# Splitting the short TensorE products of an attention block into three parts

## The chip, the cores and the metric

The kernel runs on one core of one Trainium2 chip. The metric is the device time of one execution in microseconds (us). Three runs of the kernel before gave 789.17, 789.42 and 789.59 us, median 789.42.

## The reference

One layer of a transformer trunk over 512 positions of width 2048: a normalisation, windowed attention with 32 query heads and 4 key/value heads, a gated output projection, a gated embedding, and a last normalisation. All of it is computed in single precision; the kernel writes each factor as a high and a low half and adds three products for one.

```
hn = rmsnorm(x, norm_g[i])
q, k, v, gate = split(hn @ w_in)
scores = einsum('bnqhgd,bnjhd->bnhgqj', q, kb) * HEAD_DIM ** -0.5 + bias
scores = where(mask, scores, min)
m = maximum(scores.max(-1), sink)
e = exp(scores - m)
probs = e / (e.sum(-1) + exp(sink - m))
out = einsum('bnhgqj,bnjhd->bnqhgd', probs, vb)
x = x + (out * silu(gate)) @ w_out
...
g = sigmoid(rmsnorm(x, ple_norm[i]) @ ple_gate[i])
x = x + (p[i] @ ple_proj[i]) * g
return rmsnorm(x, final_g)
```

## The kernel before

The program has four stretches. The first makes the keys, the values and the first two query tiles. The second, which the change is in, makes the other 14 query tiles and all 16 gate tiles by the generator `projections` and runs attention beside them. The third is the output projection, the fourth the gate of the embedding and the last normalisation.

A tile of the second stretch is made in 16 steps of the contraction. One step, advanced by `ksteps(1)`, is a call of `mm3`: three products whose moving side is 128x512 (lines 124, 125 and 126: high by high, low by high, high by low). These are called the long products here. Eight steps use one weight tile `wraw` of 128x1024, which ScalarE casts to its high half `whi` (`W.high`, line 107) and VectorE turns into its low half `wlo` (`W.low`, line 113). A cast is made when `splits(2)` finds fewer than two tiles ready past the one in use; it reads `at`, the number of steps issued so far.

Attention is cut into 64 blocks (4 key/value heads, 16 blocks of 32 positions each). The loop `for i in range(blocks + 3)` is a software pipeline written by hand. In turn `i` TensorE runs:

- `turn(i - 2)`, line 483: two transposes of the probabilities of block i-2 into the bank `pt`, 128x128 each;
- `weigh(i - 3)`, lines 527 and 529: the probabilities of block i-3 by the values, two products of 128x256 into the bank `o`, and a third (`own` by `DV`) for blocks whose window is cut within a tile, 48 of the 64;
- `scores(i)`, line 405: two products of queries by keys into the bank `s`, 128x288 in most blocks;
- then `todo` steps of the projections, 6 in the first 20 turns and 7 afterwards.

The first three are called the short products. Around them, in the same turn: `biased(i)` (VectorE, lines 443 to 456) adds the bias to the scores and takes the row maximum `sm`; `exps(i)` and, one turn later, `shares(i)` (ScalarE, lines 465 and 475) make the probabilities, with `inverse(i)` (VectorE, line 469) between; `high(i - 2)` (ScalarE, line 488) and `low(i - 2)` (VectorE, line 496) split the transposed probabilities into `r`; GpSimd cuts `own` out of `r` (line 507); `cross` and `merge` (lines 542 and 551) put the result away; `place(i)` (GpSimd, lines 416 to 425) clears the tile `t`. When a tile of the projections ends, its result is taken out by `evac_q` (line 277) or `evac_gate` (lines 574 and 575), issued by `ksteps` right after the last step. The scores' bank `s` exists once, the banks of `pt`, `o` and the projections twice.

TensorE and SyncE follow the order of the code throughout, and the other engines do so in this stretch: each engine's queue holds its instructions in the order in which the loop issues them. SyncE's queue carries the weight loads (line 101) and copies of weights within HBM (line 677), GpSimd's the additions onto those copies (line 679).

Of the kernel before, what the change touches and what calls it, by code (L numbers as in the profile page):

```python
# [55 lines left out]
def trunk_kernel(ctx: ExitStack, tc: tile.TileContext, a: dict):  # L56
# [26 lines left out]
    def bank(name, tag):  # L83
        return others.get(tag, psum).tile([P, 512], F32, tag=tag, name=name)
# [4 lines left out]
    class Weights:  # L89
# [13 lines left out]
        def high(self):  # L103
            i = len(self.made)
            self.load(min(i + 3, len(self.srcs)))
            hi, lo = (wpool.tile([P, WE], F32R, tag=f"w{v}", name=f"w{v}{i}") for v in ("hi", "lo"))
            nc.scalar.copy(hi, self.raw[i])  # L107
            self.made.append(tuple(t.rearrange("p (k c) -> p k c", k=8) for t in (hi, lo)))
            self.open.append((lo, self.raw[i], hi))
# [268 lines left out]
    def load_bias(kv):  # L378
        biases[kv] = apool.tile([P, P + HB], F32, tag="bias", name=f"bias{kv}", bufs=2)
        src = bass.AP(  # L380
            tensor=tdram.tensor, offset=tdram.offset + GROUP * kv * TOEP + HB, ap=[[TOEP, GROUP], [1, QB], [1, P + HB]]
        )
        nc.sync.dma_start(biases[kv], src)

    def where(i):

        kv, j = divmod(i, STEPS)
        g, half = divmod(j, 2)
        return kv, j, g, 2 * half

    def scores(i):

        kv, j, g, s = where(i)
        if j == 8 and kv + 1 < KVH:
            load_bias(kv + 1)
        key = K[kv]
        q = Q[i // 4]
        s_ps = SP[i] = spsum.tile([P, 2, S], F32, tag="w", name=f"s{i}")  # L400
        n = (HB, P)[g] if g < 2 else P + QB
        for u in range(2):
            st = q[:, (2 * i + u) % (P // QB)].rearrange("p h q -> p (h q)")
            first = 0 if g < 2 else (g - 2) * HB + (s + u) * QB
            nc.tensor.matmul(s_ps[:, u, : 2 * n], st, key[:, :, first : first + n], start=True, stop=True)  # L405

    SP = {}

    def place(i):

        kv, j, g, s = where(i)
        odd = g % 2
        n = (HB, P)[g] if g < 2 else P + QB
        t = T[i] = apool.tile([P, 2, 4 + P + HB], F32, tag="t", name=f"t{i}", bufs=4)
        sink = 193 if odd else 0
        nc.gpsimd.tensor_copy(t[:, :, sink], sinkb[:, kv : kv + 1].to_broadcast([P, 2]))
        if g == 0:
            nc.gpsimd.memset(t[:, :, 65:129], MASKED)
        elif g >= 2:
            fold = HB if odd or s else 2 * QB  # L420
            if s:
                nc.gpsimd.memset(t[:, :, 1 : 1 + (s + 1) * QB], MASKED)
            else:
                nc.gpsimd.memset(t[:, 1, 1 : 1 + QB], MASKED)
            nc.gpsimd.memset(t[:, :, 1 + s * QB + n : 1 + P + fold], MASKED)

    def views(i):

        t, odd = T[i], where(i)[2] % 2
        return (t[:, :, 65:194], t[:, :, 65:193]) if odd else (t[:, :, 0:129], t[:, :, 1:129])  # L430

    def biased(i):

        kv, j, g, s = where(i)
        odd = g % 2
        n = (HB, P)[g] if g < 2 else P + QB
        t, s_ps, bias = T[i], SP.pop(i), biases[kv][:, ::-1]
        seen, pr = views(i)
        if g < 2:
            out = pr[:, :, :n]  # L440
            for u in range(2):
                at = (2 - g) * HB - (s + u) * QB
                nc.vector.tensor_add(out[:, u], s_ps[:, u, :n], bias[:, at : at + n])
            nc.vector.tensor_add(out, s_ps[:, :, n : 2 * n], out)
        else:
            fold = HB if odd or s else 2 * QB
            w = t.shape[-1]
            at = 1 + s * QB
            out = t[:, 0, at : at + n]
            out = bass.AP(tensor=out.tensor, offset=out.offset, ap=[out.ap[0], [w + QB, 2], [1, n]])  # L450
            nc.vector.tensor_add(out, s_ps[:, :, :n], bias[:, :n].unsqueeze(1).to_broadcast([P, 2, n]))
            nc.vector.tensor_add(out, s_ps[:, :, n : 2 * n], out)
            ends = t[:, :, 1 : 1 + fold], t[:, :, 129 : 129 + fold]
            nc.vector.tensor_max(ends[odd], ends[0], ends[1])
        sm = SM[i] = apool.tile([P, 8], F32, tag="sm", name=f"sm{i}", bufs=4)
        nc.vector.tensor_reduce(sm[:, 0:2], seen, axis=AX.X, op=ALU.max, negate=True)  # L456
# [14 lines left out]
    def shares(i):  # L471

        pr, sm = views(i)[1], SM.pop(i)
        for u in range(2):
            nc.scalar.mul(pr[:, u], pr[:, u], sm[:, 4 + u : 5 + u])

    def turn(i):

        pr = views(i)[1]
        T.pop(i)  # L480
        pt = PT[i] = bank(f"pt{i}", "t")[:, :256]
        for u in range(2):
            nc.tensor.transpose(pt[:, u * P : (u + 1) * P], pr[:, u, :], ident)  # L483

    def high(i):

# [27 lines left out]
    def weigh(i):  # L514

        kv, j, g, s = where(i)
        n, b = divmod(g, 2)
        r, own = PT.pop(i)
        if j == 0:
            U[kv] = apool.tile([P, 4, S], F32, tag="u", name=f"u{kv}", bufs=2)  # L520
        if j % 2 == 0:
            O[kv] = bank(f"o{i}", "o").rearrange("p (g u e q) -> p g u e q", u=4, e=2, q=QB)
        ops = O[kv]
        out = ops[:, s : s + 2].rearrange("p g u e q -> p (g u e q)")
        first = V[0 if n == 0 else n - 1 + b][:, kv]
        for low in range(2):
            nc.tensor.matmul(out, first, r[:, low], start=low == 0, stop=own is None and low == 1)  # L527
        if own is not None:
            nc.tensor.matmul(
                out, DV[:, n - 1, b, kv * 2 * HD : (kv + 1) * 2 * HD], own, start=False, stop=True  # L530
            )

    sides = [(slice(0, 64), slice(64, 128)), (slice(64, 128), slice(0, 64))]
    TMP = {}

    def cross(i):

        kv, j, g, s = where(i)
        if s:
            tmp = TMP[i] = apool.tile([P, 4, 4, QB], F32, tag="tmp", name=f"tmp{i}", bufs=1)  # L540
            for e, (o, x) in enumerate(sides):
                nc.scalar.copy(tmp[o], O[kv][x, :, :, e, :])
# [426 lines left out]
    blocks = KVH * STEPS  # L969
    at = 0  # L970

    def ksteps(n):
        nonlocal at
        for _ in range(n):
            while len(W.made) <= min(at // 8, len(W.srcs) - 1):
                W.split()
            at += 1
            next(proj)

    def splits(ahead):  # L980
        return len(W.made) <= min(at // 8 + ahead, len(W.srcs) - 1)
# [13 lines left out]
    left = KC * len(kinds) - at  # L995

    def both(f, *v):
        fill.append((partial_of(f, *v, False), partial_of(f, *v, True)))

    for i in range(blocks + 3):  # L1000

        if i % 4 in (0, 1) and 4 <= i + 4 - i % 4 < blocks:
            both(make_q, i // 4 + 1, i % 4)
            fill.insert(0, fill.pop())
        if i in (5, 20, 36):
            both(make_key, 1 + i // 16)
        if len(due) > sum(d is gate_value for _, d in fill):
            fill.append((None, gate_value))
        now = fill[:2]
        del fill[:2]  # L1010
        while W.open:
            W.low()
        if 2 <= i < blocks + 2:
            turn(i - 2)
        if 3 <= i:
            weigh(i - 3)
        if i < blocks:
            scores(i)
            place(i)
        if 2 <= i < blocks + 2:  # L1020
            high(i - 2)
        if 3 <= i:
            cross(i - 3)
        if 1 <= i < blocks + 1:
            shares(i - 1)
        for act, dve in now:
            if act:
                act()
        if i < blocks:
            biased(i)  # L1030
        if 2 <= i < blocks + 2:
            low(i - 2)
        if 3 <= i:
            merge(i - 3)
        for act, dve in now:
            dve()
        if i < blocks:
            exps(i)
            first_chores(i)
        if splits(2):  # L1040
            W.high()
        if i < blocks:
            inverse(i)
        todo = left // (blocks + 2 - i) if i < blocks + 2 else 0
        left -= todo
        ksteps(todo)
        if i < blocks:
            for n in range(i * SUM_REST // blocks, (i + 1) * SUM_REST // blocks):
                sum_weights(SUM_START + n)
# [202 lines left out]
    for at, step in enumerate(OUT):  # L1252
# [12 lines left out]
        else:  # L1265
            p, jj, m = step
# [145 lines left out]
    for at, step in enumerate(PLE, len(OUT)):  # L1412
# [15 lines left out]
        else:  # L1428
            p, jj, m = step
# [120 lines left out]
    n = done[3]  # L1550
# [87 lines left out]
```

## Time and profile before

| | us |
|---|---|
| median of three runs | 789.42 |
| the profiled execution | 789.93 |
| its span, first to last instruction | 788.2 |
| TensorE busy | 777.6 |
| first pair of transposes of the loop to the last | 105.8 to 445.6 |

A busy share of TensorE near 100% does not by itself say that it runs at its best pace: products overlap, and a product of 128x512 is shown as 0.39 us long while the next one starts 0.23 us after it. The distance between starts is what a product costs, so the views used below are lists of instructions in order of time. There the first column is the start, the second the length, and `x2` joins two equal instructions that follow each other.

### The profile page before, as it was taken

The page shows a single profiled execution, that of the slowest core. Times are in us where ns is not written, and L with a number is a line of the kernel's source. Part 1 is how long each engine was busy: PE and PEld are TensorE (multiplying, and loading weights), DVE is VectorE, ACT ScalarE, POOL GpSimd, SP SyncE. Part 2 cuts the span into 40 slices and gives each one's busy share as a digit, 9 for nine tenths or more (in the row PEclk, how much of TensorE's full clock was granted, in tenths as well). Part 3 has the DMA queues.
Part 4 walks back from the last instruction along what each step waited for, and adds up shares of the span by engine and source line. Part 5 has one row for each costly group of instructions (what it writes and reads, how often), then busy time and mean ns, then how long its engine had stood idle before and what let it go on. Part 6 is the DMA issues. An engine that isn't in the chain of part 4 may idle for free.

```text
span 788.2 us, 11280 instructions
## 1 busy us (share of the span) xinstructions
PE 777.6 (99%) x3724; PEld 648.9 (82%) x3724; DVE 619.5 (79%) x1051; ACT 507.9 (64%) x1027; POOL 185.3 (24%) x394
## 2 busy tenths in 40 slices
PE   9999999999999999999999999999999999999995
PEld 8888888888888888888888888888888888878785
DVE  4436478887877788687887798999798988989685
ACT  5723377666666666565766656767788867867465
POOL 0201514554344414443143300100000122101000
PEclk9999999999999999999999999999999999999998
DMA  8799999999999999989997597998797999967833
GB/s 335 280 202 281 301 273 327 288 298 267 312 293 261 282 281 273 270 210 278 268 241 198 146 368 262 271 378 261 238 314 215 357 244 253 259 212 217 262 109 121
DMA packets 50634, 206.99 MB, mean 263 GB/s; under 512 B 7264, under 2 KB 8416, under 8 KB 44208
## 3 DMA queue, kind: packets, MB, share of 16 engines
q1 hardware_dynamic: 40240, 156.15, 56.3%
q0 software_dynamic: 9904, 49.61, 33.1%
q8 instruction: 29, 0.48, 0.2%
q10 hardware_dynamic: 432, 0.52, 0.2%
q14 instruction: 29, 0.24, 0.1%
HBM read 199.38 MB, written 78.69 MB: 353 GB/s over the span
## 4 chain that ended last, share of the span: by engine, by line
PE 90%; DMA 3%; DVE 3%; issue 2%; ACT 1%; ACTq 0%; DVEq 0%
PE gps L124 7%; PE gps L125 7%; PE gps L126 7%; PE qps L124 7%; PE qps L125 7%; PE qps L126 7%; PE o L126 5%; PE o L124 5%; PE o L125 5%; PE g L125 3%; PE g L126 3%; PE g L124 3%; PE s L405 2%; PE o L527 2%; PE vps L246 2%; PE pt L483 2%
## 5 line engine op out<-in xcount | busy, mean ns | idle before, releaser
L507 POOL TENSOR_SCALAR_AFFINE_SELECT own<-r 64x256 fp32r<-64x256 f32 x96 | 62.2, 648 | 163.2 <-DVE r L496 81.6
L124 PE MATMUL gps<-xh,whi 128*128 128x512 f32 x256 | 100.4, 392 | 0.0
L125 PE MATMUL gps<-xl,whi 128*128 128x512 f32 x256 | 100.0, 391 | 0.0
L126 PE MATMUL gps<-xh,wlo 128*128 128x512 f32 x256 | 99.8, 390 | 0.0
L113 DVE TENSOR_TENSOR wlo<-wraw,whi 128x1024 fp32r<-128x1024 f32 x60 | 73.8, 1231 | 26.1 <-ACT whi L107 24.7
L124 PE MATMUL qps<-xh,whi 128*128 128x512 f32 x224 | 87.5, 391 | 0.0
L125 PE MATMUL qps<-xl,whi 128*128 128x512 f32 x224 | 87.5, 390 | 0.0
L126 PE MATMUL qps<-xh,wlo 128*128 128x512 f32 x224 | 87.3, 390 | 0.0
L465 ACT ACTIVATE t<-t,sm 128x129 f32<-128x129 f32 x128 | 50.7, 397 | 50.7 <-DVE sm L456 47.5
L107 ACT CAST whi<-wraw 128x1024 fp32r<-128x1024 f32 x60 | 62.3, 1038 | 16.5 <-DMA wraw<-in_w_q 12.9
L715 DVE TENSOR_TENSOR blo<-braw,bhi 128x1024 fp32r<-128x1024 f32 x43 | 52.5, 1224 | 17.4 <-ACT bhi L714 17.4
L714 ACT CAST bhi<-braw 128x1024 fp32r<-128x1024 f32 x43 | 45.0, 1048 | 30.6 <-PE g L126 9.0
L715 DVE TENSOR_TENSOR blo<-ring,bhi 128x1024 fp32r<-128x1024 f32 x48 | 58.2, 1220 | 4.3 <-ACT bhi L714 3.8
L714 ACT CAST bhi<-ring 128x1024 fp32r<-128x1024 f32 x48 | 50.2, 1049 | 17.1 <-PE o L126 13.3
L125 PE MATMUL g<-blo,fhg 128*128 128x512 f32 x148 | 58.1, 392 | 0.5 <-DVE blo L715 0.5
L124 PE MATMUL g<-bhi,fhg 128*128 128x512 f32 x148 | 58.0, 392 | 0.0
L126 PE MATMUL g<-bhi,flg 128*128 128x512 f32 x148 | 57.6, 390 | 0.0
L488 ACT CAST r<-pt 128x256 fp32r<-128x256 f32 x64 | 23.8, 372 | 51.6 <-PE pt L483 51.3
L126 PEld LDWEIGHTS gps<-xh,wlo 128*128 128x128 f32 x256 | 48.1, 188 | 10.5
L124 PEld LDWEIGHTS gps<-xh,whi 128*128 128x128 f32 x256 | 48.1, 188 | 9.1
L125 PEld LDWEIGHTS gps<-xl,whi 128*128 128x128 f32 x256 | 48.1, 188 | 8.7
L126 PEld LDWEIGHTS qps<-xh,wlo 128*128 128x128 f32 x224 | 42.1, 188 | 9.0
(298 smaller groups left out, 2033.4 us busy)
## 6 DMA issues: line engine op xcount, KB each, us to landing
w_out<-in_w_out POOLq DMA_DIRECT2D x32, 512.0 KB, 9.2
wraw<-in_w_gate_in SPq DMA_DIRECT2D x32, 512.0 KB, 7.1
ring<-w_out SPq DMA_DIRECT2D x32, 512.0 KB, 5.3
wraw<-in_w_q SPq DMA_DIRECT2D x28, 512.0 KB, 8.9
braw<-in_ple_gate SPq DMA_DIRECT2D x22, 512.0 KB, 5.3
ring<-in_w_out SPq DMA_DIRECT2D x18, 512.0 KB, 5.5
ple_gate<-in_ple_gate SPq DMA_DIRECT2D x16, 512.0 KB, 9.5
ple_gate<-in_ple_gate POOLq DMA_DIRECT2D x16, 512.0 KB, 8.1
```

The lines of the kernel that those rows point to most:

```text
L107: nc.scalar.copy(hi, self.raw[i])
L113: nc.vector.tensor_sub(lo, raw, hi.bitcast(F32))
L124: nc.tensor.matmul(ps, sh, mh, start=first, stop=False, skip_group_check=more)
L125: nc.tensor.matmul(ps, sh, ml, start=False, stop=False, skip_group_check=more)
L126: nc.tensor.matmul(ps, sl, mh, start=False, stop=last, skip_group_check=more)
L246: nc.tensor.matmul(v_ps[t], h[:, c], both[:, :, 256:512], start=f, stop=e, skip_group_check=True)
L405: nc.tensor.matmul(s_ps[:, u, : 2 * n], st, key[:, :, first : first + n], start=True, stop=True)
L465: nc.scalar.activation(su, su, AF.Exp, bias=sm[:, u : u + 1], accum_out=sm[:, 2 + u : 3 + u])
L488: nc.scalar.copy(r[:, 0], PT[i])
L507: nc.gpsimd.affine_select(out=cols(own[places[g % 2 ^ low]]), in_=cols(r[here, low].bitcast(F32)), pattern=[[sign * QB, 2], [0, GROUP], [s ...
L714: nc.scalar.copy(hi, raw)
L715: nc.vector.tensor_sub(lo, raw, hi.bitcast(F32))
```

## The change

The three functions that issue the short products become generators that yield after each product, and the loop runs them with steps of the projections between:

```
 def scores(i):
...
             nc.tensor.matmul(s_ps[:, u, : 2 * n], st, key[:, :, first : first + n], start=True, stop=True)
+            yield
 def turn(i):
...
             nc.tensor.transpose(pt[:, u * P : (u + 1) * P], pr[:, u, :], ident)
+            yield
 def weigh(i):
...
         for low in range(2):
             nc.tensor.matmul(out, first, r[:, low], start=low == 0, stop=own is None and low == 1)
+            yield
         if own is not None:
             nc.tensor.matmul(
                 out, DV[:, n - 1, b, kv * 2 * HD : (kv + 1) * 2 * HD], own, start=False, stop=True
             )
+            yield
...
         while W.open:
             W.low()
-        if 2 <= i < blocks + 2:
-            turn(i - 2)
-        if 3 <= i:
-            weigh(i - 3)
+        todo = left // (blocks + 2 - i) if i < blocks + 2 else 0
+        left -= todo
+        shorts = []
+        shorts += [turn(i - 2)] if 2 <= i < blocks + 2 else []
+        shorts += [weigh(i - 3)] if 3 <= i else []
+        shorts += [scores(i)] if i < blocks else []
+        for n, short in enumerate(shorts):
+            for m, _ in enumerate(short):
+                if todo > 1 and m == 1 and n < len(shorts) - 1:
+                    ksteps(1)
+                    todo -= 1
         if i < blocks:
-            scores(i)
             place(i)
...
         if i < blocks:
             inverse(i)
-        todo = left // (blocks + 2 - i) if i < blocks + 2 else 0
-        left -= todo
         ksteps(todo)
```

After the second transpose and after the second product of `weigh` one step, three long products, is issued. The third product of `weigh`, where there is one, then stands with the scores. The number of steps in each turn, and each product, stays as it was. Two steps out of six or seven now stand ahead of the turn's work on the other engines.

TensorE's queue in turn 39, before (`pt37` belongs to block 37, `o36` to block 36, `s39` to block 39; the long products write `qps14`):

```order
L126 MATMUL qps14_3325<-xh2_213,wlo36_3246 128x512
L483 MATMUL pt37_3338<-ident_83,t37_3224 128x128 x2
L527 MATMUL o36_3341<-r36_3285,V0_715 128x256 x2
L529 MATMUL o36_3341<-own36_3298,DV_745 128x256
L405 MATMUL s39_3345<-k2_2168,q9_2925 128x288 x2
L124 MATMUL qps14_3325<-xh3_244,whi36_3245 128x512
L125 MATMUL qps14_3325<-xl3_245,whi36_3245 128x512
L126 MATMUL qps14_3325<-xh3_244,wlo36_3246 128x512
L124 MATMUL qps14_3325<-xh4_278,whi36_3245 128x512
```

The same place after the change:

```order
L126 MATMUL qps14_3325<-xh2_213,wlo36_3199 128x512
L484 MATMUL pt37_3338<-ident_83,t37_3236 128x128 x2
L124 MATMUL qps14_3325<-xh3_244,whi36_3198 128x512
L125 MATMUL qps14_3325<-xl3_245,whi36_3198 128x512
L126 MATMUL qps14_3325<-xh3_244,wlo36_3199 128x512
L529 MATMUL o36_3344<-r36_3291,V0_715 128x256 x2
L124 MATMUL qps14_3325<-xh4_278,whi36_3198 128x512
L125 MATMUL qps14_3325<-xl4_279,whi36_3198 128x512
L126 MATMUL qps14_3325<-xh4_278,wlo36_3199 128x512
L532 MATMUL o36_3344<-own36_3304,DV_745 128x256
L405 MATMUL s39_3351<-k2_2178,q9_2931 128x288 x2
L124 MATMUL qps14_3325<-xh5_312,whi36_3198 128x512
```

Seven short products in a row have become 2, 2 and 3, and the scores stand six long products later.

On VectorE, the end of turn 36 and the start of turn 37, before (`wlo35` is the low half of weight tile 35, `t36` and `t37` are the blocks' scores, `rawq3` the query tile taken out, `k3` the last key):

```order
L315 TENSOR_TENSOR k3_3164<-kt1_714,k3_3164 64x512 x2
L469 RECIPROCAL sm36_3170<-sm36_3170 128x2
L277 TENSOR_TENSOR rawq3_0_3192<-qps12_3069,rb_91 128x256
L277 TENSOR_TENSOR rawq3_1_3194<-qps12_3069,rb_91 128x256
L113 TENSOR_TENSOR wlo35_3183<-wraw35_3002,whi35_3182 128x1024
L451 TENSOR_TENSOR t37_3224<-s37_3221,bias2_2402 128x2x144
```

The same work after the change, now at the start of turn 36:

```order
L470 RECIPROCAL sm35_3119<-sm35_3119 128x2
L113 TENSOR_TENSOR wlo35_3128<-wraw35_3008,whi35_3127 128x1024
L277 TENSOR_TENSOR rawq3_0_3160<-qps12_3037,rb_91 128x256
L277 TENSOR_TENSOR rawq3_1_3162<-qps12_3037,rb_91 128x256
L452 TENSOR_TENSOR t36_3167<-s36_3164,bias2_2408 128x2x144
L453 TENSOR_TENSOR t36_3167<-s36_3164,t36_3167 128x2x144
```

The low half of tile 35 is made one turn earlier, because `splits(2)` now sees two steps more, and the query tile, which ends in the second step of turn 36, is taken out ahead of block 36's scores. The same happens to other weight tiles: 10, 13, 16, 19, 22, 28, 29, 35, 36, 42, 43, 49, 50, 56 and 57 are cast one turn earlier, and their loads move with them on SyncE's queue. GpSimd's queue is in the same order as before.

More of the change, by code (lines that the diff above doesn't have):

```diff
@@ L405, in scores @@
             nc.tensor.matmul(s_ps[:, u, : 2 * n], st, key[:, :, first : first + n], start=True, stop=True)
+            yield
     SP = {}
@@ L483, in turn @@
             nc.tensor.transpose(pt[:, u * P : (u + 1) * P], pr[:, u, :], ident)
+            yield
     def high(i):
@@ L527, in weigh @@
             nc.tensor.matmul(out, first, r[:, low], start=low == 0, stop=own is None and low == 1)
+            yield
         if own is not None:
@@ L531, in weigh @@
             )
+            yield
     sides = [(slice(0, 64), slice(64, 128)), (slice(64, 128), slice(0, 64))]
@@ L1012, in trunk_kernel @@
             W.low()
[L1013 to L1016, printed above, removed]
+        todo = left // (blocks + 2 - i) if i < blocks + 2 else 0
+        left -= todo
+        shorts = []
+        shorts += [turn(i - 2)] if 2 <= i < blocks + 2 else []
+        shorts += [weigh(i - 3)] if 3 <= i else []
+        shorts += [scores(i)] if i < blocks else []
+        for n, short in enumerate(shorts):
+            for m, _ in enumerate(short):
+                if todo > 1 and m == 1 and n < len(shorts) - 1:
+                    ksteps(1)
+                    todo -= 1
         if i < blocks:
-            scores(i)
             place(i)
@@ L1043, in trunk_kernel @@
             inverse(i)
-        todo = left // (blocks + 2 - i) if i < blocks + 2 else 0
-        left -= todo
         ksteps(todo)
```

## The prediction

> **What bounds the kernel now.** I read the page's first line, then TensorE's waits, the busy time by stretch, and last TensorE's instructions one by one.
>
> ```profile
> PE 777.6 (99%) x3724; PEld 648.9 (82%) x3724; DVE 619.5 (79%) x1051; ACT 507.9 (64%) x1027; POOL 185.3 (24%) x394
> ```
>
> ```profile
> PE warm_ps L145 <- PEq L1628: 0.8, 1, 0.8
> PE g L125 <- DVE blo L715: 0.5, 1, 0.5
> PE qps L234 <- ACT xh L217: 0.2, 1, 0.2
> ```
>
> ```profile
> 97.00:272.00 175.00, 175.00 (x872) 146.94 (x871) 139.63 (x317) 116.86 (x324) 73.78 (x166) 1.00 1.01 288
> 272.00:446.00 174.00, 174.00 (x864) 146.02 (x864) 136.76 (x292) 110.59 (x299) 63.69 (x153) 1.00 0.92 246
> ```
>
> The three rows in the middle are all that TensorE waits for in the whole span, 1.5 us, and none of it is in the attention loop. In the last two rows, the loop (97 to 446 us), TensorE is busy for all of 349 us at the full granted clock (the 1.00), while VectorE works 276.4 us of it. So in this stretch time is lost or won in two ways only: the distance from one product's start to the next changes, or a wait appears that isn't there now. There is no wait left to remove.
>
> The distances come from the list of TensorE's instructions. Turns 39 and 40, with the first three long products of each kept and a few further on:
>
> ```profile
> 299.67 0.39 PE L126 MATMUL qps<-xh,wlo 128*128 128x512 f32 x1
> 299.90 0.38 PE L483 MATMUL pt<-ident,t 128*128 128x128 f32 x2
> 300.03 0.48 PE L527 MATMUL o<-r,V 128*128 128x256 f32 x2
> 300.35 0.28 PE L529 MATMUL o<-own,DV 128*128 128x256 f32 x1
> 300.47 0.43 PE L405 MATMUL s<-k,q 128*128 128x288 f32 x2
> 300.74 0.40 PE L124 MATMUL qps<-xh,whi 128*128 128x512 f32 x1
> ...
> 301.43 0.39 PE L124 MATMUL qps<-xh,whi 128*128 128x512 f32 x1
> ...
> 305.54 0.38 PE L483 MATMUL pt<-ident,t 128*128 128x128 f32 x2
> ...
> 307.98 0.39 PE L125 MATMUL qps<-xl,whi 128*128 128x512 f32 x1
> ...
> 310.93 0.40 PE L126 MATMUL qps<-xh,wlo 128*128 128x512 f32 x1
> 311.16 0.38 PE L483 MATMUL pt<-ident,t 128*128 128x128 f32 x2
> ```
>
> From 307.98 to 310.93 there are 13 steps from one long product to the next, 2.95 us: 0.2269 us each, the undisturbed pace. The seven short products take 300.74 - 299.90 = 0.84 us. A turn with 21 long products should then take 0.84 + 21 x 0.2269 = 5.605 us. It takes 305.54 - 299.90 = 5.64 and 311.16 - 305.54 = 5.62. So one group of short products costs some 0.035 and 0.015 us, mean 0.025, beyond its own length, **in the long products next to it**. The first three after the group show it: 300.74 to 301.43 is 0.69, where three undisturbed ones take 0.681.
>
> **The change part by part.** It removes and adds no instruction; it moves products, and with them work on other engines.
>
> *The short products themselves: 0.* What they cost for being short is the transposes' weight load:
>
> ```profile
> 299.90 0.14 PEld L483 LDWEIGHTS pt<-ident,t 128*128 128x128 f32 x1
> 300.01 0.30 PEld L527 LDWEIGHTS o<-r,V 128*128 128x128 f32 x2
> ```
>
> The load for the second transpose starts at 299.90, with the first transpose, and the load for the values at 300.01, with the second. Each load begins when the product ahead of it begins and takes 0.11 us; by its columns a transpose would take 128/512 of 0.2269 = 0.057. So each transpose costs 0.11 whatever follows. That this holds for a long product behind it is seen later in the program, where transposes stand between long products:
>
> ```profile
> 601.53 0.36 PEld L1130 LDWEIGHTS tp<-ident,x 128*128 128x128 f32 x3
> 601.86 0.19 PEld L124 LDWEIGHTS i<-spare,ih 128*128 128x128 f32 x1
> 601.97 0.19 PEld L125 LDWEIGHTS i<-spare,ih 128*128 128x128 f32 x1
> ```
>
> The long product's load starts at 601.86, three transposes of 0.11 after 601.53, and so with the fourth; the next load, which marks the long product's real start, comes at 601.97, again 0.11 later. The pair of transposes stays a pair, and the products of 256 and 288 columns, whose 0.11 to 0.13 us covers a load, pay nothing today. So moving long products between them saves nothing.
>
> The Trainium skill says otherwise in one place (TensorE: Matmul & The Clock Gate, "Step-by-step: what each phase is for"): the queue's reorder window pulls weight loads ahead of products still running when they go to the background buffer. Read as more than one load ahead, a short product's load would hide behind the long ones now put next to it; in the rows above each load waits for the product just before it to start, so the trace bears out one load ahead and no more. What the other reading would give is the second rival.
>
> *The breaks.* A turn has one change from long to short and back now, and three afterwards. Turns 3 to 63 get two more each, turns 2, 64 and 65 one each: 2 x 61 + 3 = 125 more pieces of three long products with short ones at both ends. No piece of three exists in this trace. The nearest are pieces of six between transposes:
>
> ```profile
> 593.79 0.60 PE L1130 MATMUL tp<-ident,x 128*128 128x128 f32 x4
> ...
> 597.44 1.03 PE L1130 MATMUL tp<-ident,x 128*128 128x128 f32 x8
> ...
> 598.55 0.39 PE L125 MATMUL i<-blo,ih 128*128 128x512 f32 x1
> ...
> 601.53 0.60 PE L1130 MATMUL tp<-ident,x 128*128 128x128 f32 x4
> ...
> 602.20 0.39 PE L125 MATMUL i<-spare,ih 128*128 128x512 f32 x1
> ...
> 603.36 0.49 PE L1130 MATMUL tp<-ident,x 128*128 128x128 f32 x3
> ```
>
> Eight transposes and a long product take 1.11 us (597.44 to 598.55), four and one 0.67, so a transpose takes 0.11, between 0.108 and 0.110 within the rounding of the rows. From 593.79 to 603.36, 9.57 us, there are 24 transposes and 30 long products in five pieces of six. Take off 24 x 0.109 = 2.62: 6.95 us are left, 0.2318 a long product, against 0.2269. That is 0.005 each, 0.029 for a piece of six, the same as the 0.025 of a group in the loop with 21 behind it. The slow ones are thus the products nearest to a break.
>
> For a piece of three I take 3 x 0.005 = 0.015 us. Below that lies the 0.01 of the loop's first three (0.69 against 0.681); above it a piece of three that costs as much as one of six, 0.029, with the rounding 0.033. That it costs nothing, or that smaller groups disturb less than the group of seven does now, is not excluded: then at most today's 0.025 in 64 turns, 1.6 us, is saved. The term: **125 x 0.015 = 1.9 us**, with 125 x 0.01 = 1.3 and 125 x 0.033 = 4.1 as its near ends, and -1.6 as the far one. The last part of each turn, values and scores or scores alone, keeps the 12 or 15 long products behind it and today's 0.025, which is no change.
>
> *The scores later: 0, covered by slack.* They stand six long products later, 6 x 0.2269 and two breaks, 1.4 us. Queued behind them on VectorE are the row maximum, `low`, `merge`, and the next `wlo`; behind the maximum on ScalarE the exponentials. VectorE has room, and already waits for scores:
>
> ```profile
> DVE t L451 <- PE s L405: 26.0, 26, 3.0
> DVE t L443 <- PE s L405: 4.3, 9, 0.9
> ```
>
> In 35 of the 64 turns it stands idle ahead of `biased`; there its work moves 1.4 us back against the transposes. What TensorE takes from it, with the least slack that I find in the trace:
>
> ```profile
> 133.82 0.50 POOL L507 TENSOR_SCALAR_AFFINE_SELECT own<-r 64x256 fp32r<-64x256 f32 x1 [1.74 <-DVE r L496]
> ```
>
> ```profile
> 133.28 0.41 DVE L496 TENSOR_TENSOR r<-pt,r 128x256 fp32r<-128x256 f32 x1
> 290.14 1.22 DVE L113 TENSOR_TENSOR wlo<-wraw,whi 128x1024 fp32r<-128x1024 f32 x1
> ```
>
> ```profile
> 134.73 0.48 PE L527 MATMUL o<-r,V 128*128 128x256 f32 x2
> 135.05 0.28 PE L529 MATMUL o<-own,DV 128*128 128x256 f32 x1
> 292.13 0.39 PE L126 MATMUL qps<-xh,wlo 128*128 128x512 f32 x1
> ```
>
> `own` ends at 134.32 and is used at 135.05: 0.73 us. It can come 1.4 later, but its product moves back by the same 1.4 (two parts), so the slack stays. `r` ends at 133.69 and its second product begins about 0.2 after 134.73: 1.2 us; it loses 1.4 - 0.7 = 0.7 and 0.5 is left. `wlo` of tile 35 ends at 291.36 and is used at 292.13: 0.77 us, the narrowest; just this one is made a turn earlier after the change. The bank `s` gets free as long before the next scores as now, since both move. I cost all this at nothing; if one such cover is gone, TensorE stands for some tenths of a us in that turn.
>
> *Tiles taken out earlier on VectorE and ScalarE, and loads moved on SyncE: 0.* `evac_q` and `evac_gate` that fall into the first two steps now run ahead of `biased`, in the time that VectorE waits for the scores, and two steps of long products are still ahead of the bank's next use. The 15 weight loads that move go to an earlier place in SyncE's queue, ahead of a copy.
>
> The sum against the profiled execution: 789.93 + 1.9 = 791.8. That execution is 0.5 above the median; against the median 789.42 + 1.9 = **791.3 us**.
>
> **The rivals.** *The small groups don't disturb.* A group of two or three short products may pass without slowing its neighbours. Then nothing is added, and at the far end today's 0.025 a turn goes too: 789.4 to 787.8, middle 788.6. For it: I don't know what the slow products wait for, and no group here is as small. Against it: four transposes disturb as much as seven products.
>
> *Weight loads hide behind long products: not slower.* If the load behind the second transpose of a pair were pulled ahead when a long product follows, 0.11 - 0.057 = 0.05 us would be saved in 64 turns, 3.4 us: 786.0. It decides when the load of a long product starts before the transpose ahead of it does. Against it: the load at 601.86.
>
> *The scores' shift becomes a wait.* VectorE or GpSimd falls behind in the turns where it does more (key splits, tiles taken out ahead of the scores), and TensorE waits for `r`, `own` or `wlo`. With 0.2 us in a fifth of the turns, 13 x 0.2 = 2.6, on top of the breaks: 793.9. For it: slacks of 0.5 to 0.8. Against it: most of them move along, as worked out.
>
> **How the numbers follow.** Forecast 66%, its own range 790.5 to 793.3 (1.1 to 3.9 added); no disturbance 15%; hidden loads 7%; new waits 12%. A change of 0.2%, 1.6 us, is about what a measurement of this kernel can tell from none: under 787.8 is faster, over 791.0 slower. The forecast lies near that bound: with 0.0126 us a piece it is met, so of its 66% I count 52 slower and 14 same; the first rival 10 same and 5 faster, the second faster, the third slower. Faster 0.12, same 0.24, slower 0.64. The range for 8 in 10 leaves out the hidden loads and a little at each end: 788.0 to 794.2.
>
> **What would show it.** In the new trace a turn of three parts and 21 long products lasts about 5.65 to 5.67 us where it lasts 5.62 and 5.64 now; each piece of three takes 0.69 to 0.70 us from its first start to the next short product's real start; TensorE's waits still hold no row of the loop; the load behind the second transpose starts with that transpose. A turn of the old length makes the first rival right; a transpose pair that takes less than 0.22 us up to the long product's start the second; a row `PE o` or `PE qps` waiting for VectorE or GpSimd the third. Outside the loop every stretch should keep its length.

## The result, and the profile after

The changed kernel took 791.77 us in the median of nine runs (790.69 to 793.12), the kernel before 789.52 in nine. The ratio is 1.0026, with a 95% interval of 1.0018 to 1.0035: slower by a quarter of a per cent, where 1.9 us or 0.24% were forecast.

The page's first line, and all of TensorE's waits in the profiled execution after the change:

```profile
PE 779.8 (99%) x3724; PEld 648.7 (82%) x3724; DVE 621.6 (79%) x1051; ACT 504.5 (64%) x1027; POOL 191.6 (24%) x394
```

```profile
PE warm_ps L145 <- PEq L1636: 0.8, 1, 0.8
PE qps L234 <- ACT xh L217: 0.2, 1, 0.2
```

TensorE's work is the same 3724 products, busy 779.8 us in place of 777.6, and the view of the waits still has no row from the loop. (One short wait does hide from it; it comes below.)

The spans of the two profiled executions, 788.2 and 790.2, don't give what the change did alone: the stretch before the loop and the one after it vary from run to run. The loop itself can be cut out, from the start of the projections' first long product to that of the last. The two rows of the kernel before, then of the changed one:

```profile
71.27 0.40 PE L124 MATMUL qps<-xh,whi 128*128 128x512 f32 x1
...
450.69 0.39 PE L126 MATMUL gps<-xh,wlo 128*128 128x512 f32 x1
```

```profile
71.75 0.40 PE L124 MATMUL qps<-xh,whi 128*128 128x512 f32 x1
...
453.47 0.39 PE L126 MATMUL gps<-xh,wlo 128*128 128x512 f32 x1
```

The loop grew from 379.41 (the rows give 379.42; the trace holds whole nanoseconds) to 381.72 us, **by 2.31 us**. The way in took 0.48 us more and the way out 0.85 less. The kernel before varies as much by itself: in a second trace of it they took 0.35 more and 1.10 less.

Turns 39 and 40 after the change, in the list of TensorE's instructions:

```profile
301.81 0.38 PE L484 MATMUL pt<-ident,t 128*128 128x128 f32 x2
301.95 0.47 PE L124 MATMUL qps<-xh,whi 128*128 128x512 f32 x1
302.26 0.39 PE L125 MATMUL qps<-xl,whi 128*128 128x512 f32 x1
302.49 0.40 PE L126 MATMUL qps<-xh,wlo 128*128 128x512 f32 x1
302.72 0.40 PE L529 MATMUL o<-r,V 128*128 128x256 f32 x2
302.97 0.40 PE L124 MATMUL qps<-xh,whi 128*128 128x512 f32 x1
303.20 0.39 PE L125 MATMUL qps<-xl,whi 128*128 128x512 f32 x1
303.43 0.39 PE L126 MATMUL qps<-xh,wlo 128*128 128x512 f32 x1
303.66 0.28 PE L532 MATMUL o<-own,DV 128*128 128x256 f32 x1
303.77 0.43 PE L405 MATMUL s<-k,q 128*128 128x288 f32 x2
304.04 0.40 PE L124 MATMUL qps<-xh,whi 128*128 128x512 f32 x1
...
307.48 0.38 PE L484 MATMUL pt<-ident,t 128*128 128x128 f32 x2
```

The turn takes 307.48 - 301.81 = 5.67 us, where the two quoted of the kernel before took 5.64 and 5.62. From the first transpose to the values it is 0.91: two transposes of 0.108 and three long products of 0.23, not 0.2267, each. From 302.97 to 303.66 the next three take 0.69 in place of 0.68.

The same subtraction made for the new pieces of three (all but the one of turn 2), with the undisturbed 0.2267 taken off for each product, gives a mean of 0.018 us behind transposes (63 pieces) and 0.012 behind values (61), 1.83 us together. A piece is counted here from the real start of its first long product, which the next weight load marks, so that a wait ahead of it isn't counted in.

**The rest is a wait.** Turn 13 in the list of TensorE of the changed kernel, and what ScalarE and VectorE did in turn 12 and after it:

```profile
159.70 0.39 PE L125 MATMUL gps<-xl,whi 128*128 128x512 f32 x1
159.92 0.39 PE L126 MATMUL gps<-xh,wlo 128*128 128x512 f32 x1
160.35 0.62 PE L484 MATMUL pt<-ident,t 128*128 128x128 f32 x2
160.73 0.48 PE L124 MATMUL gps<-xh,whi 128*128 128x512 f32 x1
```

```profile
155.27 1.04 ACT L107 CAST whi<-wraw 128x1024 fp32r<-128x1024 f32 x1
158.20 0.60 ACT L579 ACTIVATE gps<-gate 128x512 f32<-128x512 f32 x1 [1.89 <-DVE gate L578]
158.73 0.37 ACT L490 CAST r<-pt 128x256 fp32r<-128x256 f32 x1
159.13 0.75 ACT L546 COPY tmp<-o 64x256 f32<-64x256 f32 x2
159.90 0.70 ACT L476 ACTIVATE t<-t,sm 128x128 f32<-128x128 f32 x2
```

```profile
156.34 1.23 DVE L113 TENSOR_TENSOR wlo<-wraw,whi 128x1024 fp32r<-128x1024 f32 x1 [0.78 <-ACT whi L107]
157.48 0.68 DVE L578 TENSOR_TENSOR gate<-gps,rb 128x512 f32<-128x512 f32 x1
```

The transposes start 0.43 after the long product ahead of them, not 0.23, and the pair then takes 160.73 - 160.35 = 0.38 up to the next row, not the usual 0.14. They wait for the probabilities of block 11, which ScalarE scales from 159.90 to 160.60. ScalarE is late because a gate tile ended in the moved steps of turn 12: its Tanh (line 579) stands ahead of that turn's other work, the scaling included. ScalarE stood idle for 1.89 us ahead of it, until VectorE, which first made the low half of a weight tile, had the gate tile taken out (line 578). The view of the waits shows no row for it, because a product of 128x512 is drawn 0.39 us long and covers the gap.

### The profile page after: what moved, and what is told of

Its sections match the earlier page's. It is cut to its first block, busy times and chain, and to the rows that moved or that the text cites. A ratio compares the mean times of both kernels' runs of the same rounds, so it can differ in the third digit from the quotient of the medians.

```text
span 790.2 us, 11290 instructions
## 1 busy us (share of the span) xinstructions
PE 779.8 (99%) x3724; PEld 648.7 (82%) x3724; DVE 621.6 (79%) x1051; ACT 504.5 (64%) x1027; POOL 191.6 (24%) x394
## 4 chain that ended last, share of the span: by engine, by line
PE 95%; DVE 2%; DMA 1%; issue 1%; ACT 1%; SPq 0%; ACTq 0%; DVEq 0%
PE gps L124 8%; PE gps L125 7%; PE gps L126 7%; PE qps L126 7%; PE qps L124 7%; PE qps L125 7%; PE o L126 5%; PE o L124 5%; PE o L125 5%; PE g L125 4%; PE g L126 4%; PE g L124 4%; PE s L405 2%; PE o L529 2%; PE pt L484 2%; PE vps L246 2%
## 5 line engine op out<-in xcount | busy, mean ns | idle before, releaser
L509 POOL TENSOR_SCALAR_AFFINE_SELECT own<-r 64x256 fp32r<-64x256 f32 x96 | 71.3, 742 | 164.7 <-DVE r L498 107.2
L124 PE MATMUL gps<-xh,whi 128*128 128x512 f32 x256 | 103.9, 406 | 0.0
L124 PE MATMUL qps<-xh,whi 128*128 128x512 f32 x224 | 90.2, 403 | 0.0
L124 PE MATMUL o<-bhi,fho 128*128 128x512 f32 x124 | 48.4, 390 | 0.0
```

Source lines behind the costliest of these rows:

```text
L124: nc.tensor.matmul(ps, sh, mh, start=first, stop=False, skip_group_check=more)
L509: nc.gpsimd.affine_select(out=cols(own[places[g % 2 ^ low]]), in_=cols(r[here, low].bitcast(F32)), pattern=[[sign * QB, 2], [0, GROUP], [s ...
```

## The experiments

All loop lengths below run from the first long product of the projections to the last, in one trace each.

**The kernel before, once more.**

> The kernel before once more, to see how well the length of the loop repeats: 379.4 us within 0.1, from the first long product of the projections to the last. If it differs by more, the loop lengths of single traces can't carry the comparisons of some tenths of a us.

Measured: loop 379.41 us, within a nanosecond of the first trace, where the time before the loop differed by 0.35 us. These are two traces, and of one kernel; from here on, differences of tenths of a us between the loops of single traces are read as real.

**The tiles taken out late** (e1): the changed kernel's order on TensorE, with `evac_q` and `evac_gate` put back to the end of the turn's other work.

```
...
+        between.append(i)
         for n, short in enumerate(shorts):
...
+        between.clear()
...
             inverse(i)
+        while put_off:
+            put_off.pop(0)()
         ksteps(todo)
```

> The changed kernel's order on TensorE, but a projection tile that ends in one of the two moved steps is taken out (evac_q, evac_gate) at the end of the turn's other work, as in the kernel before. In the changed kernel the loop, from the first long product of the projections to the last, lasts 381.72 us against 379.41, and one wait stands in it: the transposes of turn 13, from 159.92 on, come some 0.4 us late, because ScalarE's Tanh of a gate tile stands ahead of the scaling of the probabilities. Theory (breaks and this wait): the wait goes, the pieces of three stay, loop 381.3 us, 1.9 above the kernel before. Rival (the whole loss comes from work of the other engines that moved): the loop falls back further, under 380.5.

Measured: loop 381.27 us, time ratio 1.0024 (1.0015 to 1.0034). The same turn 13:

```profile
159.62 0.40 PE L126 MATMUL gps<-xh,wlo 128*128 128x512 f32 x1
159.85 0.38 PE L484 MATMUL pt<-ident,t 128*128 128x128 f32 x2
159.99 0.48 PE L124 MATMUL gps<-xh,whi 128*128 128x512 f32 x1
```

```profile
154.96 1.03 ACT L107 CAST whi<-wraw 128x1024 fp32r<-128x1024 f32 x1
155.90 0.36 ACT L490 CAST r<-pt 128x256 fp32r<-128x256 f32 x1
157.00 0.75 ACT L546 COPY tmp<-o 64x256 f32<-64x256 f32 x2 [0.74 <-PE o L532]
157.77 0.70 ACT L476 ACTIVATE t<-t,sm 128x128 f32<-128x128 f32 x2
```

No Tanh stands between, the scaling is done at 158.47, and the transposes start 0.23 after the product ahead of them. That takes off 381.72 - 381.27 = 0.45 us. What is left is 1.86 over the kernel before, and the pieces of three sum to 1.83 here. The two agree so well by some luck, for two smaller changes cancel in the trace: the long products in the last part of each turn lose 0.37 us more in all than they do in the kernel before, and the short products together take 0.35 less (50.67 us where they took 51.02).

**The steps first** (e2): the two steps stand ahead of the short products, which stay together. The work of the other engines moves as in the changed kernel; no break is added.

```
+        for _ in shorts[1:]:
+            if todo > 1:
+                ksteps(1)
+                todo -= 1
+        for short in shorts:
+            run(short)
```

> The two steps stand ahead of the short products, which stay one group: no new break between long and short products, but the tiles are taken out and the weights cast as early as in the changed kernel. Theory (breaks): loop 379.4 us as in the kernel before, up to 0.5 more if a wait on ScalarE like that of turn 13 comes back; time ratio to the kernel before 0.999 to 1.001. Rival (moved work of the other engines costs the time): loop near 381.7, ratio 1.0026.

Measured: loop 379.95 us, ratio 1.0005 (0.9996 to 1.0014). The 0.54 over the kernel before is one wait, in turn 14, for `own` from GpSimd; the view of the waits gives it 0.3 us, again because the rest lies under a product:

```profile
PE o L532 <- POOL own L509: 0.3, 1, 0.3
```

Moved work of the other engines without breaks costs one wait and nothing else. The rival's 381.7 falls.

**One break** (e3): the step behind the transposes alone.

```
-                if todo > 1 and m == 1 and n < len(shorts) - 1:
+                if todo > 1 and m == 1 and n == 0 and len(shorts) > 1:
```

> The changed kernel with the step behind the transposes alone; values and scores stay together. Theory (breaks): 63 pieces of three at 0.0175 us, 1.1 in all, loop 380.5 us, and up to 0.5 more if a wait of the kind of turn 13 comes. Rival (a group of short products costs by its size, so two parts cost as one): 379.4.

Measured: loop 380.35 us, 0.93 over the kernel before, with 63 pieces that sum to 1.11; ratio 1.0008 (0.9999 to 1.0017), which by itself can't tell it from none. That is 0.18 less than the pieces' sum. The trace shows where it came back: the short products of the loop take 50.82 us in all, where they took 51.02 in the kernel before.

**One long product, and six, in each place** (e6, e4). In e6 `projections` yields after each product; in e4 each place has two steps.

```
                 if todo > 1 and m == 1 and n < len(shorts) - 1:
+                    thirds(1)
+                    todo -= n == 0
+        todo += part > 0
```

```
+                if todo > 2 and m == 1 and n < len(shorts) - 1:
+                    ksteps(2)
+                    todo -= 2
```

> The changed kernel with one long product instead of three in each of the two places; the rest of the step follows behind the scores. Theory (0.005 us for each long product near a break): 125 x 0.005 = 0.6, loop 380.0 us. Rival (a fixed amount for each break): 125 x 0.015 = 1.9, loop 381.3 us. The scores come only 0.45 us later and a tile ends in the moved part never in most turns, so the wait of turn 13 should not come.

> The changed kernel with two steps, six long products, in each of the two places. Theory as in the prediction (each long product near a break is slower by 0.005 us, up to the whole 0.025 to 0.03 of a recovery): a piece of six costs 0.025 to 0.034, 125 pieces 3.1 to 4.2, loop 382.5 to 383.6 without waits. Rival (a break costs a fixed amount at its edges, however many long products stand in the piece): 0.015 a piece as now, loop 381.3 to 381.8. As the scores come 2.7 us later than in the kernel before, waits may come on top; they would show as transposes or values that start late.

Measured, e6: loop 380.23 us, 0.81 over the kernel before; ratio 1.0013 (1.0004 to 1.0022). Its 124 pieces of one long product sum to 0.95 us, 0.0077 each. Measured, e4: loop 387.14; ratio 1.0101 (1.0086 to 1.0117). Its 124 pieces of six sum to 3.37, 0.027 each. With 0.0147 for three (e1), the cost of a break grows with the number of long products behind it, in the mean about 0.005 us each, up to six; a fixed amount for each break falls. The single pieces don't follow the mean: of the 63 pieces of six behind transposes 19 cost 0.015 to 0.017, no more than a piece of three, and the others 0.025 to 0.036. In the kernel before, too, the long products behind a group are back at their undisturbed pace after two of them in some turns (0.012 us lost), and in others only after eight (up to 0.047).

The other 4.4 us of e4 are waits in the main, of which the view shows 2.8. TensorE's waits in its loop, and the longest of them:

```profile
PE pt L484 <- ACT t L476: 2.5, 3, 1.4
PE o L529 <- DVE r L498: 0.3, 1, 0.3
```

```profile
162.54 0.40 PE L126 MATMUL gps<-xh,wlo 128*128 128x512 f32 x1
164.36 0.62 PE L484 MATMUL pt<-ident,t 128*128 128x128 f32 x2 [1.42 <-ACT t L476]
```

With the scores 2.7 us later the transposes start up to 1.6 us late (1.42 of it idle in the view), because the scaled probabilities are not ready. So the cover that the changed kernel lives on does end, not far behind it.

**Each short product apart** (e5): one step behind every short product, while steps last.

```
-                if todo > 1 and m == 1 and n < len(shorts) - 1:
+                if todo > 1:
```

> The changed kernel with one step behind every short product, the two transposes and the two scores apart from each other too, as far as the turn's steps reach. Theory (breaks): 0.0175 us for a piece of three behind a transpose, 0.012 behind another product, some 0.075 a turn and 4.6 in all, less 1.5 because the last stretch of a turn is 3 long products in place of 12 or 15: loop near 382.5 us without waits; a transpose still takes 0.108 us up to the real start of the long product behind it. Rival (the load behind a lone transpose is hidden by the long products around it): a transpose takes about 0.06 and the loop is up to 6 us shorter than that. The scores come over 3 us later than in the kernel before, so waits of several us in all will come on top, as with six long products in a piece.

Measured, in a single execution: 811.22 us, loop 400.98. The expectation for the length missed by far, because the waits are much longer than "several us" (the probabilities alone 11.0 us in 12 waits). The question it was made for is answered. One of its 128 transposes, in the list of weight loads:

```profile
200.19 0.14 PEld L484 LDWEIGHTS pt<-ident,t 128*128 128x128 f32 x1
200.42 0.19 PEld L124 LDWEIGHTS qps<-xh,whi 128*128 128x128 f32 x1
200.53 0.19 PEld L125 LDWEIGHTS qps<-xl,whi 128*128 128x128 f32 x1
```

The load for the long product starts with the transpose, at 200.42, and the load after it, which marks that product's real start, 0.11 later. Each of the 128 stands alone between long products; 113 of them take 0.108 to 0.114 us up to the real start of the product behind them, and the other 15, which follow a wait or fall into the slower clock described at the end, take longer. None takes less, so no load is hidden.

**Halves** (e7): the kernel before, with one long product in the middle of each turn's stretch cut into two of 256.

```
+                if (m, k) in halved:
+                    for c2 in (slice(0, 256), slice(256, 512)):
+                        nc.tensor.matmul(ps[:, c2], wh[:, k % 8, :], xh[k][:, c2], start=False, stop=False)
...
```

> The kernel before, with one long product in the middle of each turn's stretch cut into two of 128x256 with the same weights: 66 breaks with no wait, no transpose and no other operand. Each half has the 0.013 us that a product of 256 takes over half of one of 512 (0.120 against 0.113), so 66 x 0.013 = 0.9 at least. Theory (any product of another width disturbs the long ones near it): 0.025 to 0.04 more a turn, loop 379.4 + 0.9 + 1.7 to 2.6 = 382.0 to 382.9. Rival (the slowing comes from what the short products wait for, or from the transposes' weight loads): loop 380.3.

Measured: loop 381.61 us, ratio 1.0031 (1.0019 to 1.0043). The loop is 2.20 over the kernel before, less than expected and far from the rival's 0.9. Around one pair of halves:

```profile
304.23 0.40 PE L124 MATMUL qps<-xh,whi 128*128 128x512 f32 x1
...
304.92 0.40 PE L952 MATMUL qps<-xh,whi 128*128 128x256 f32 x2
305.15 0.40 PE L953 MATMUL qps<-xl,whi 128*128 128x512 f32 x1
...
306.08 0.39 PE L126 MATMUL qps<-xh,wlo 128*128 128x512 f32 x1
306.31 0.39 PE L124 MATMUL qps<-xh,whi 128*128 128x512 f32 x1
```

The two halves take 305.15 - 304.92 = 0.23 us, in the mean of the 66 pairs 0.2325. So a pair is only 0.006 longer than one long product, not 0.013, and the halves' own length accounts for 66 x 0.0058 = 0.38 us. The remaining 1.82, 0.028 a break, is within the 0.025 to 0.04 expected; what the expectation had too large was the length of the halves. From 305.15 to 306.31 five long products take 1.16, 0.232 each, with no transpose and no product of the attention among them.

## Why the prediction was right

**What bounds the kernel**: right. TensorE's pace and new waits were the only two ways, and both appeared, 1.86 and 0.45 us (e1).

**The short products themselves, 0**: right in its reason, that no load is hidden. The pair of transposes still takes 0.216 us up to what follows, and in e5 none of the 128 lone transposes takes under 0.108. The rival of the hidden weight load is shown to be wrong. So is, for this kernel, the reading of the Trainium skill (TensorE: Matmul & The Clock Gate, "Step-by-step: what each phase is for") by which more than one load is pulled ahead. The term was not quite nothing: in e1 all short products together take 0.35 us less. This was hidden by luck, for the last part of each turn, which the prediction left at "today's 0.025, which is no change", lost 0.37 more. That 0.025 came from two turns; over the loop of the kernel before the mean is 0.033, and in e1 it is 0.038.

**The breaks, 125 x 0.015 = 1.9 us**: right in where the time is lost and how much. The pieces cost 1.83 us without the wait (e1, 124 of them), 0.0147 each; they differ by kind, 0.0175 behind transposes and 0.012 behind values. The step from pieces of six to pieces of three, by 0.005 a product, was an assumption; the means of e6 (0.0077 for one) and e4 (0.027 for six) bear it out on both sides, though single pieces scatter about it. The rival by which small groups don't disturb falls with e3, where the part split off holds two transposes only.

**The scores later, 0**: right for `r`, `own` and `wlo`, the three that were checked. The slack that was not looked at, that of the scaled probabilities for the transposes, is the one that ran out.

**Tiles taken out earlier on VectorE and ScalarE, 0**: this step failed, by 0.45 us. It covered the earlier work by VectorE's wait for the scores, and said nothing of what stands behind the Tanh on ScalarE's queue. There the scaling that the transposes of the next turn need stood behind it, and ScalarE idled 1.89 us. So something like the third rival came true in one turn of 64, through an engine and an operand that it did not name, beside the forecast and not in place of it.

The total, 2.25 us between the medians of nine runs, is 0.35 above the forecast, inside its own range.

What stays open is why long products near a product of another width are slower. The e7 pieces exclude the transposes, the waits and the attention's operands as its only cause; extra weight loads come with every break there too, so width and load count were not told apart.

## What to carry to other kernels

Where TensorE never waits, count what a reordering does to the distances between its starts: a short product can cost time in its neighbours, here in the mean about 0.005 us for each of the next six or so, and splitting one group into three pays it three times. Putting long products beside short ones hides a weight load only if the trace shows loads that start earlier than the product just ahead. When a step is moved, list what stands behind each of its instructions on every engine, and look for the new wait in distances between starts too, since the view of waits misses what lies under a product's drawn length.

## What the runs showed of the hardware

In e5 two long waits were followed by a slower clock. Three stretches of that kernel: the wait of turn 13, a stretch soon after it, and the time after that. Each row has the busy time of TensorE, its weight loads, VectorE, ScalarE and GpSimd; the last three figures are the granted clock, the DMA share and GB/s.

```profile
160.70:163.20 2.50, 0.37 (x3) 0.07 (x2) 2.38 (x8) 2.16 (x6) 0.78 (x2) 1.00 0.99 206
164.40:167.60 3.20, 3.20 (x10) 2.52 (x9) 1.59 (x3) 2.68 (x7) 1.65 (x4) 0.51 1.04 298
168.00:172.00 4.00, 4.00 (x22) 3.31 (x21) 2.54 (x6) 0.85 (x5) 0.54 (x1) 1.00 1.04 325
```

TensorE idled for 2.1 us, up to 163.13. The clock stayed at 1.00 for over a us after that, then stood at half from 164.5 to 167.9, with long products 0.43 us apart. About half of these 3.4 us was thus lost on top of the wait. The only other wait of over 2 us in that run, which ended at 416.7, was followed by the same: half the clock from 417.1 to 420.5. In e4, whose longest idle stretch was 1.42 us, the loop has no product at that distance.
